# Softmax sums of an attention loop: the reciprocals' way through DRAM, and the place of two reads in the DMA queue

## The chip, the cores and the metric

The kernel runs on one core of one Trainium2 chip. A core has a matrix engine (TensorE, PE in the profile, with its weight loads as PEld), VectorE (DVE), ScalarE (ACT), GpSimd (POOL) and a queue engine, SyncE (SP), which issues nearly all of this kernel's transfers. The metric is the device time in microseconds (us) of one execution. The time before the change is 2631.48 us, the median of three runs (2627.51 to 2632.87).

## The reference

One layer of a diffusion transformer over 1024 latent tokens of width 1024, with 256 context tokens in front: a half-step feed-forward part, then a convolution branch beside an attention branch, merged by gates, then a second feed-forward part and a final norm. All is float32. The change lies in the attention, where 8 query heads in 2 groups read 1280 keys (256 of the context, 1024 latent), each with head width 128:

```
s = einsum('btkgd,blkd->bkgtl', q, k) * HEAD_DIM ** -0.5
p = softmax(s, axis=-1)
o = einsum('bkgtl,blkd->btkgd', p, v)
```

## The kernel before

Products are made from float32 values split into a high and a low part, as high by high, high by low and low by high: three matmuls stand for one product, and each operand costs a cast (ACT or POOL) and a subtraction (DVE or POOL). The kernel runs in stages: first feed-forward part, input projections, heads, attention, the branches' outputs and merge, second feed-forward part. In most stages a planner with a cost model orders the instructions. The attention loop is written out by hand: while `strict` is set, every engine, and SP with its transfers, keeps the order of the program text.

**The loop** has 16 units, one for each head and each half (512) of the queries. A unit has five steps, and step `t` of the loop does four things: scores and exponentials of 128 queries of the current unit (in the unit's first four steps), the turning of two key tiles of 128 of the unit before (`turn`, `placed_parts`), the product with the values for the two tiles turned in the step before (`values`), and some matmuls of the convolution branch's output projection (`fillers`, with their weight and input loads). Other work is put into four places of a step by `later(t, place, ...)`: `first`, `mid`, `after` and `end`, in this order; the fillers run between `after` and `end`. Things put into one place run in the order in which they were put there, unit by unit.

**Turning the probabilities.** The value product needs keys on the partitions. For query tiles 2 and 3 of a unit, and for the context keys, TensorE turns them. For query tiles 0 and 1 the exponentials of the latent keys lie in two tiles `pb` (128 by 1024), and each goes this way (`place`): VectorE turns its 32 by 32 blocks in place; four transfers write it to DRAM as `turned`, in pieces of 64 numbers (256 bytes); one transfer reads it back as `placed`, in pieces of 1024 bytes, with keys on the partitions. Below, the write and the read of a unit's first `pb` are write A and read A, those of the second write B and read B. With `t0` a unit's first step, write A stands at the end of `t0+3` and read A at the first place of `t0+4`; write B stands at the end of `t0+4` and read B at the first place of `t0+5`. `placed` is first used in step `t0+7` (A) and `t0+9` (B).

**The sums.** The exponentials are not divided before the value product. VectorE sums them (`rsum`, 128 partitions by 4 query tiles); `inverse` takes the reciprocals (`rinv`), writes these 512 numbers to DRAM (`rinvd`) and reads them back as one row of 512 on all 128 partitions (`rrow`); `output` multiplies the unit's output, which has queries along the row, by that row on POOL (on VectorE for the last unit). The write of `rinv` stands at the end of `t0+6`, which is step 1 of the next unit, and the row's read at the end of `t0+9`; the product comes in step `t0+12`. In DRAM the row is in the order of the queries, so the write

```
sp.dma_start(out=row.rearrange("(j p) -> p j", p=P), in_=rinv[:])
```

puts down 512 single numbers of 4 bytes.

**SP's queue** takes its transfers in order, and one that waits for its data holds all behind it. A read of something that was written to DRAM waits until the write has landed. Around the change the order for unit `n`, with the fillers' loads (`g`, `raw`, `y`) and stores (`zd`) in between, is: write A(n), read A(n), `rrow`(n-1), write B(n), read B(n), `rinvd`(n), write A(n+1).

Of the kernel before, what the change touches and what calls it, by code (L numbers as in the profile page):

```python
# [18 lines left out]
P = 128  # L19
# [32 lines left out]
def tile_dit_layer(  # L52
# [44 lines left out]
    act, dve, pool, pe, sp = (Engine(e) for e in (nc.scalar, nc.vector, nc.gpsimd, nc.tensor, nc.sync))  # L97
# [11 lines left out]
    def uniq(s):  # L109
        n_tiles[0] += 1  # L110
        return f"{s}_{n_tiles[0]}"
# [4 lines left out]
    def ttile(name, n=512, dt=F32):  # L116
        t = tpool.tile([P, 512], dt, tag="t", name=uniq(name))
        return t[:, :n]

    def small(name, n, dt=F32):  # L120
        return spool.tile([P, n], dt, tag=f"s{n}_{name}", name=uniq(name))
# [64 lines left out]
    def col(name, k=0):  # L186
        o = voff[name] + k
        return cols[:, o : o + 1]
# [856 lines left out]
    def fetch_tokens(ch):  # L1045
        s, o, n = ch
        src = x[0] if s == "l" else ctxt[0]
        toks = []
        for j in range(n // P):
            t = atile("xtok")  # L1050
            load(t[:], src[o + j * P : o + (j + 1) * P, :], True)
            toks.append(t)
        return toks
# [41 lines left out]
    t0 = fetch_tokens(C0)  # L1095
# [47 lines left out]
    for k in range(4):  # L1143
        if k % 2:
            half1.shifted(h0[k][:, 0], k, xh[k])
        else:
            dve.tensor_scalar(
                out=h0[k][:, 0], in0=xh[k], scalar1=gain1["l"][:, k : k + 1], scalar2=modl[:, k : k + 1],
# [131 lines left out]
    for j in range(NH):  # L1280
        half1.side = side(j) if j >= SIDE_FROM else None
        u, c = half1.next_first()
        v, b = half1.second(u)
# [115 lines left out]
    for i in range(KD):  # L1399
# [6 lines left out]
        for ch, bg, gc in mixed():  # L1406
# [4 lines left out]
            for j in (0, 2):  # L1411
# [3 lines left out]
                    out=ya, in0=u[:, a + j - 1 : b + j - 1], scalar=col(f"w{j}", i), in1=ya, op0=ALU.mult, op1=ALU.add  # L1415
# [112 lines left out]
    def q_of(hd, ch):  # L1528
        return q_pairs[hd // 2, ch][:, hd % 2]
# [92 lines left out]
    class Unit:  # L1622
# [84 lines left out]
            matmul(po, vh, pts[:, 1], start=False, stop=(kt == 9))  # L1707

        def inverse(self):
            rinv = small("rinv", 4)  # L1710
            dve.reciprocal(out=rinv[:], in_=self.rsum[:])
            yield
            row = dram.tile([512], F32, name=uniq("rinvd"))
            sp.dma_start(out=row.rearrange("(j p) -> p j", p=P), in_=rinv[:])
            yield
            self.rows = ttile("rrow")
            sp.dma_start(out=self.rows, in_=row.partition_broadcast(P))
            yield

        def output(self, by=None):  # L1720
            of = q_of(self.hd, self.ch)
            v = lambda t, by: t[:, :256].rearrange(by, i=4, q=2)
            act.copy(out=v(of, "p (q i c) -> p q i c"), in_=v(self.po, "p (i q c) -> p q i c"))
            act.copy(out=of[:, 256:], in_=self.po[:, 256:])
            yield
            (by or pool).tensor_mul(out=of, in0=of, in1=self.rows)
            yield

    m_hi, m_lo = {}, {}
# [39 lines left out]
    def later(t, when, f, *args):  # L1769
        todo.setdefault((t, when), []).append((f, args))  # L1770
# [74 lines left out]
    for n, u in enumerate(units):  # L1845
        t0, t1 = n * STEPS_OF_UNIT, (n + 1) * STEPS_OF_UNIT
        if n:
            later(t0 - 2, "mid", u.begin, split_apart)
        for j in range(2):
            place = u.place(j)  # L1850
            later(t0 + 2 + j, "after", run, place, 1)
            later(t0 + 3 + j, "end", run, place, 1)
            later(t0 + 4 + j, "first", run, place, 1)
        inverse, output = u.inverse(), u.output(dve if n == len(units) - 1 else None)
        later(t1 + LAG, "after", run, inverse, 1)
        later(t1 + LAG, "end", run, inverse, 1)
        later(t1 + LAG + 3, "end", run, inverse, 1)
        later(t1 + LAG + 6, "mid", run, output, 1)
        later(t1 + LAG + 6, "end", run, output, 1)
        if n % 2 and n < len(units) - 1:  # L1860
            later(last - 1 + u.hd // 2, "after", split_output, u.hd, C0, True)
            later(last + 1 + u.hd // 2, "after", split_output, u.hd, C1, True)
# [5 lines left out]
    turned = {}  # L1868
# [45 lines left out]
    first = fast.norm0()  # L1914
    fast.gain = norm_gain("gain3", 6, "g3")["l"]
    for ch in (C0, C1):
        o = ch[1]
        for d in range(KD):
# [7 lines left out]
                out=xs(d, ch), in0=ps, scalar=modl[:, 40 + d : 41 + d], in1=xs(d, ch), op0=ALU.mult, op1=ALU.add  # L1926
# [12 lines left out]
        out=gf[:], in0=cols[:, voff["gf"] : voff["gf"] + 8], scalar1=math.sqrt(D), scalar2=None, op0=ALU.mult  # L1939
# [47 lines left out]
    for j in range(NH):  # L1987
# [3 lines left out]
        v, b = fast.second(u)  # L1991
# [81 lines left out]
```

## Time and profile before

| what | value |
|---|---|
| median of three runs | 2631.48 us (2627.51 to 2632.87) |
| the profiled execution, its own time | 2631.88 us |
| its span, first to last instruction | 2630.1 us |
| busy: PE, DVE, ACT, POOL | 2588.5, 2003.6, 1184.4, 605.7 us |
| granted TensorE clock, mean | 0.995 |
| attention: first and last reciprocals of sums | 1457.5 and 1783.8 us of the span |
| DMA: moved, mean rate | 418.27 MB, 159 GB/s |

An instruction's row has its line, engine, operation, the tiles it writes and reads, how many there are, busy time in us, the mean of one in ns, and the engine's idle time just before with what ended it. All of this kernel's instructions go through one helper and so have one line, L90; they are told apart by their tiles. A matmul's end is modelled, so a busy TensorE is not one at its peak. Rows of waits say which engine waited for whom: us in total, how many times, the longest. Rows of a stretch (from:to) have its length, the busy time of PE, PEld, DVE, ACT and POOL with their instructions, the granted clock, the share of time in which the 16 DMA engines were busy, and GB/s. Rows in order of time have start, duration, engine, and in brackets the idle time before and what ended it.

### The profile page before, as it was taken

How to read it: one execution, taken by the hardware profiler on the slowest of the kernel's cores; microseconds unless marked ns; L12 is line 12 of the kernel's file. 1: busy time of each engine (PE TensorE's matmuls, PEld its weight loads, DVE VectorE, ACT ScalarE, POOL GpSimd, SP SyncE). 2: the span in 40 equal slices, each digit the busy share in tenths (PEclk: the TensorE clock that was granted, in tenths of full speed). 3: DMA queues.
4: the chain of work that ended last, by engine and by line, in shares of the span. 5: the costliest groups of instructions: out<-in, count | busy, mean ns of one | idle time of the engine just before them, and what ended most of it. 6: DMA issues, size and time to landing. Idle time of an engine off the chain costs nothing. (4 is left out here: it accounts for less than half of the span.)

```text
span 2630.1 us, 35610 instructions
## 1 busy us (share of the span) xinstructions
PE 2588.5 (98%) x12387; PEld 2152.3 (82%) x12387; DVE 2003.6 (76%) x3381; ACT 1184.4 (45%) x2480; POOL 605.7 (23%) x497
## 2 busy tenths in 40 slices
PE   8999999999999999999999999998999999999998
PEld 5888898888888888888888877876888888888888
DVE  5888876878897879977788776775457786667996
ACT  6533454333554642333345676763237223334553
POOL 0135201221010034333022344432000442321100
PEclk9999999999999999999999999999999999999999
DMA  9666475335973364533523787886425653227831
GB/s 325 205 206 199 141 213 171 121 116 204 309 182 116 129 205 157 175 120 99 198 69 95 136 173 142 153 146 178 156 85 176 193 176 96 89 83 277 199 83 65
DMA packets 470763, 418.27 MB, mean 159 GB/s; under 512 B 100134, under 2 KB 353208, under 8 KB 470584
## 3 DMA queue, kind: packets, MB, share of 16 engines
q1 hardware_dynamic: 462936, 401.33, 51.7%
q0 software_dynamic: 7648, 14.68, 3.3%
q8 instruction: 97, 1.59, 0.3%
q14 instruction: 82, 0.67, 0.1%
HBM read 327.23 MB, written 88.64 MB: 158 GB/s over the span
## 5 line engine op out<-in xcount | busy, mean ns | idle before, releaser
L90 PE MATMUL ps<-r,wl 128*128 128x512 f32 x5196 | 1197.0, 390 | 2.7 <-ACT r L90 1.7
L90 PEld LDWEIGHTS ps<-r,wl 128*128 128x128 f32 x5196 | 972.3, 188 | 205.9 <-ACT r L90 1.9
L90 ACT CAST wl<-sum 128x512 fp32r<-128x512 f32 x218 | 133.9, 621 | 316.6 <-PE ps L90 242.7
L90 ACT CAST wl<-raw 128x512 fp32r<-128x512 f32 x287 | 177.7, 620 | 207.2 <-PE ps L90 157.4
L90 DVE TENSOR_TENSOR wl<-raw,wl 128x512 fp32r<-128x512 f32 x287 | 206.0, 721 | 62.7 <-ACT wl L90 61.2
L90 POOL TENSOR_TENSOR sum<-raw 128x512 f32<-128x512 f32 x55 | 80.9, 1472 | 707.5 <-DVE wl L90 224.3
L90 DVE TENSOR_TENSOR wl<-sum,wl 128x512 fp32r<-128x512 f32 x218 | 193.4, 888 | 42.8 <-ACT wl L90 41.6
L90 DVE TENSOR_REDUCE m<-ps 128x1 f32<-128x512 f32 (+1 forms) x192 | 114.8, 602 | 82.9 <-PE ps L90 65.2
L90 DVE TENSOR_TENSOR u<-u,ps 128x512 f32<-128x512 f32 x186 | 126.7, 681 | 33.8 <-PE ps L90 33.8
L90 DVE SCALAR_TENSOR_TENSOR macc<-rawm,silu_r,macc 128x512 f32<-128x512 f32 x165 | 134.3, 835 | 16.7 <-DMA rawm<-in_w_mod_dram 16.3
L90 ACT CAST rh<-hid 128x512 fp32r<-128x512 f32 x132 | 81.8, 622 | 135.9 <-PE ps L90 110.2
L90 POOL TENSOR_TENSOR pts<-placed,pts 128x256 fp32r<-128x256 f32 x128 | 94.7, 762 | 199.5 <-ACT pts L90 120.5
L90 POOL TENSOR_TENSOR sum<-raw,sum 128x512 f32<-128x512 f32 x55 | 76.6, 1393 | 271.8 <-DVE wl L90 267.3
L90 PE MATMUL ps<-rh,wl 128*128 128x512 f32 x360 | 122.1, 390 | 0.0
L90 PE MATMUL ps<-wh,r 128*128 128x512 f32 x384 | 120.4, 393 | 0.0
L90 ACT CAST wh<-raw 128x512 fp32r<-128x512 f32 (+1 forms) x83 | 66.0, 796 | 111.6 <-PE ps L90 76.8
L90 DVE TENSOR_TENSOR rl<-hid,rh 128x512 fp32r<-128x512 f32 x132 | 90.8, 692 | 26.4 <-ACT rh L90 14.9
L90 PE MATMUL ps<-y,wc 128*128 128x512 f32 x384 | 102.8, 394 | 2.0 <-DVE y L90 1.2
L90 PE MATMUL ps<-rh,wh 128*128 128x512 f32 x300 | 102.3, 389 | 0.0
L90 PE MATMUL ps<-kl,qs 128*128 128x512 f32 x384 | 99.9, 395 | 1.9 <-ACT pb L90 1.8
L90 POOL DMA_DIRECT2D ws<-in_ffn_w_out_dram x30 | 35.5, 1232 | 252.5 <-DMA ws<-in_ffn_w_out_dram 64.2
L90 POOL TENSOR_TENSOR sum<-sum,raw 128x512 f32<-128x512 f32 x55 | 87.0, 1581 | 6.0 <-PE ps L90 4.0
(339 smaller groups left out, 5144.9 us busy)
## 6 DMA issues: line engine op xcount, KB each, us to landing
raw<-in_ffn_w_in_dram SPq DMA_DIRECT2D x131, 512.0 KB
raw<-in_ffn_w_out_dram SPq DMA_DIRECT2D x72, 512.0 KB
rawm<-in_w_mod_dram SPq DMA_DIRECT2D x136, 256.0 KB
raw<-in_w_in_dram SPq DMA_DIRECT2D x64, 512.0 KB
hid<-hd SPq DMA_DIRECT2D x40, 512.0 KB
ucd<-uc SPq DMA_DIRECT2D x33, 512.0 KB
turned<-pb SPq DMA_DIRECT2D x128, 128.0 KB
placed<-turned SPq DMA_DIRECT2D x32, 512.0 KB
```

The lines of the kernel that those rows point to most:

```text
L90: inst = getattr(self.engine, name)(*args, **kw)
```

## The change

Three edits. In `inverse` the four columns of reciprocals are put into columns 0, 32, 64 and 96 of a 128 by 128 tile, which is filled with ones first; VectorE turns its 32 by 32 blocks, after which the numbers lie in partitions 0, 32, 64 and 96, 128 in each; these four rows of 512 bytes are written to DRAM. The row in DRAM is then in the order (i, j, r), where query `j*128 + i*32 + r` is meant, and in `output` the product takes both operands through views that put this right. In the loop, reads A and B move from the first place of their steps to the end of the same steps.

```diff
         def inverse(self):
-            rinv = small("rinv", 4)
-            dve.reciprocal(out=rinv[:], in_=self.rsum[:])
+            turned = ttile("rinv", P)
+            dve.memset(turned, 1.0)
+            dve.reciprocal(out=turned[:, ::32], in_=self.rsum[:])
+            dve.transpose(out=turned, in_=turned)
             yield
             row = dram.tile([512], F32, name=uniq("rinvd"))
-            sp.dma_start(out=row.rearrange("(j p) -> p j", p=P), in_=rinv[:])
+            sp.dma_start(out=row.rearrange("(i f) -> i f", i=4), in_=turned[::32])
             yield
             self.rows = ttile("rrow")
             sp.dma_start(out=self.rows, in_=row.partition_broadcast(P))
...
-            (by or pool).tensor_mul(out=of, in0=of, in1=self.rows)
+            v = lambda t, by: t.rearrange(by, i=4, j=4)
+            of, rows = v(of, "p (j i r) -> p j i r"), v(self.rows, "p (i j r) -> p j i r")
+            (by or pool).tensor_mul(out=of, in0=of, in1=rows)
             yield
...
             place = u.place(j)
             later(t0 + 2 + j, "after", run, place, 1)
             later(t0 + 3 + j, "end", run, place, 1)
-            later(t0 + 4 + j, "first", run, place, 1)
+            later(t0 + 4 + j, "end", run, place, 1)
```

In SP's queue the order becomes: write A(n), the fillers' loads of step `t0+4`, `rrow`(n-1), read A(n), write B(n), the fillers' loads of step `t0+5`, read B(n), `rinvd`(n), write A(n+1).

## The prediction

> **What bounds the kernel now.** The page's head comes first:
>
> ```profile
> span 2630.1 us, 35610 instructions
> PE 2588.5 (98%) x12387; PEld 2152.3 (82%) x12387; DVE 2003.6 (76%) x3381; ACT 1184.4 (45%) x2480; POOL 605.7 (23%) x497
> L90 PE MATMUL ps<-kl,qs 128*128 128x512 f32 x384 | 99.9, 395 | 1.9 <-ACT pb L90 1.8
> ```
>
> TensorE sets the end, so the change is worth what it takes out of TensorE's waits, no more. It touches attention alone, so next I took the busy times of the stretch from the first reciprocals to the last turned keys, then, narrower, the granted clock:
>
> ```profile
> 1457.00:1806.00 349.00, 328.70 (x1647) 267.92 (x1648) 252.62 (x545) 242.12 (x720) 142.48 (x155) 0.98 0.82 147
> ...
> 1584.00:1588.00 4.00, 4.00 (x18) 3.51 (x17) 0.00 (x0) 3.46 (x9) 3.63 (x3) 0.57 0.34 80
> 1747.00:1752.00 5.00, 4.95 (x15) 3.85 (x16) 2.70 (x7) 3.61 (x12) 2.73 (x4) 0.66 0.57 170
> 1788.00:1803.00 15.00, 10.41 (x28) 7.52 (x29) 9.00 (x11) 8.40 (x20) 10.13 (x8) 0.66 0.64 198
> ```
>
> TensorE stands for 349.0 - 328.7 = 20.3 us of this stretch. In three places its clock is lowered as well: 4 x 0.43 + 5 x 0.34 + 15 x 0.34 = 8.5 us of work lost. About 0.6 us of that falls into a wait counted already, so 7.9. Who ended the waits (TensorE's rows, then ScalarE's, then SP's, same stretch):
>
> ```profile
> PE ps L90 <- ACT pts L90: 7.5, 2, 5.0
> PE pt L90 <- DVE pts L90: 6.0, 6, 2.5
> PE ps L90 <- ACT pc L90: 2.9, 3, 1.8
> PE ps L90 <- ACT pb L90: 1.8, 1, 1.8
> PE ps L90 <- DVE y L90: 1.2, 1, 1.2
> PE po L90 <- ACT pts L90: 1.1, 2, 0.7
> ```
>
> ```profile
> ACT pts L90 <- DMA placed<-turned: 37.0, 12, 7.3
> ACT pb L90 <- DMA turned<-pb: 2.7, 1, 2.7
> ```
>
> ```profile
> SPq L90 <- DMA turned<-pb: 145.5, 53, 9.5
> ```
>
> TensorE waits for ScalarE, and ScalarE waits for `placed`, 37.0 us in 12 of 32 reads; while it stands, its exponentials (`pc`, `pb`) stand too. `placed` is late because SP waits 145.5 us for the landing of `turned`. Why that takes so long is seen in SP's order, unit 0 above the dots, units 2 and 3 below:
>
> ```profile
> 1440.01 2.19 SPq L90 DMA_DIRECT2D turned<-pb  x4
> 1444.50 0.39 SPq L90 DMA_DIRECT2D placed<-turned  x1
> ...
> 1501.98 0.38 SPq L90 DMA_DIRECT2D placed<-turned  x1
> 1502.46 0.45 SPq L90 DMA_DIRECT2D rinvd<-rinv  x1
> 1503.96 2.64 SPq L90 DMA_DIRECT2D turned<-pb  x4
> 1515.38 0.38 SPq L90 DMA_DIRECT2D placed<-turned  x1
> 1516.83 0.43 SPq L90 DMA_DIRECT2D rrow<-rinvd  x1
> 1517.36 2.76 SPq L90 DMA_DIRECT2D turned<-pb  x4
> 1523.26 0.38 SPq L90 DMA_DIRECT2D placed<-turned  x1
> ```
>
> Write A of unit 3 ends its issue at 1506.6 and read A starts at 1515.38: 8.8 us to land. Write B, of the same size and shape, takes 1523.26 - 1520.12 = 3.1 us; write A of unit 0, with no write of sums ahead of it, 2.3. What precedes the slow one alone is `rinvd`, 512 pieces of 4 bytes. The DMA's columns say the same:
>
> ```profile
> 1440.00:1445.00 5.00, 4.44 (x21) 3.43 (x20) 3.02 (x6) 3.22 (x9) 2.39 (x1) 1.00 0.62 108
> ...
> 1506.00:1515.00 9.00, 8.55 (x42) 6.43 (x41) 6.74 (x17) 4.74 (x17) 2.19 (x4) 1.00 1.11 46
> 1517.00:1523.00 6.00, 6.00 (x31) 4.86 (x31) 4.47 (x11) 4.98 (x14) 3.13 (x3) 1.00 1.05 324
> ```
>
> After the 4-byte pieces the engines count as fully busy and move 46 GB/s; around write B, as busy, 324. So the small pieces hold up what comes behind them. Two kinds of lateness follow: a read B issued just ahead of `rinvd` is not done for 10.7 us (issued 1501.98, cast at 1512.70), and a read A starts late behind its slow write, then takes 4.1 us (1785.58 to 1789.66, last unit):
>
> ```profile
> 1512.70 0.71 ACT L90 CAST pts<-placed 128x256 fp32r<-128x256 f32 x2 [3.93 <-DMA placed<-turned]
> ...
> 1789.66 0.71 ACT L90 CAST pts<-placed 128x256 fp32r<-128x256 f32 x2 [7.25 <-DMA placed<-turned]
> ...
> 1785.58 0.38 SPq L90 DMA_DIRECT2D placed<-turned  x1
> ```
>
> [...]
>
> **The change part by part.** *The write of four rows.* 16 x 512 = 8192 pieces of 4 bytes become 64 of 512 bytes. No write of this trace has this form; its cost lies between nothing and that of today's write. I take nothing, since four pieces are few beside the 2048 of a write B, which lands in 3.1 us. Write A then lands 2.3 to 3.1 us after its issue instead of 8.8, and read A can start some 6 us earlier; read B is no longer held up. What this releases, term by term:
>
> - TensorE's waits for ScalarE, 7.5 + 1.1 + 2.9 + 1.8 = 13.3 us: all taken. Bounds: half of it, if reads stay at the edge, to all.
> - Of the 6.0 us for VectorE's `pts`, the wait of 2.5 us: VectorE's row shows that it had stood 7.82 us for ScalarE's casts of `oh`, which stood behind `placed` in ScalarE's order. The other five are VectorE's own queue. Bounds 0 to 6.0.
>
> ```profile
> 1792.42 5.27 DVE L90 TENSOR_TENSOR ol<-q,oh 128x512 fp32r<-128x512 f32 x3 [7.82 <-ACT oh L90]
> ```
>
> - The clock, 7.9 us: each of the three places follows such a wait. [...]
> - What waits don't show. A matmul's row is 395 ns, but 384 of them add only 99.9 us of busy time, 260 ns each: in a gap the modelled end covers some 0.13 us. For the 9 waits above, 1.2 us; bounds 0 to 2.
>
> [...]
>
> Sum of gains: 13.3 + 2.5 + 7.9 + 1.2 = 24.9 us.
>
> *The work added on VectorE and POOL.* The rows nearest to it:
>
> ```profile
> L90 DVE RECIPROCAL rinv<-rsum x16: 167/168/171, 1457.5 to 1783.8; 128x4 f32<-128x4 f32 x16
> L90 DVE STREAM_TRANSPOSE pb<-pb 128x1024 f32<-128x1024 f32 x32 | 39.5, 1235 | 0.0
> L90 POOL TENSOR_TENSOR q<-q,rrow x15: 1282/1297/1734, 1481.3 to 1794.3; 128x512 f32<-128x512 f32 x15
> L90 POOL TENSOR_TENSOR hsw<-xb,rope x48: 456/790/1716, 1291.6 to 1423.1; 128x256 f32<-128x256 f32 x32, 128x128 f32<-128x128 f32 x16
> ```
>
> The reciprocal stays, 0.17 us. The turn of 128 columns costs between 1235/8 = 154 ns and that plus the 168 of a small operation; I take 0.2. The fill, not in the trace on this engine at this size, is put at 0.05 to 0.3 by the same rows; I take 0.15. That is 0.35 us for a unit, 5.6 in all, on an engine busy for 252.62 of 349 us:
>
> ```profile
> DVE m L90 <- PE ps L90: 58.7, 93, 4.3
> 1544.50:1566.25 21.75, 20.55 (x108) 16.89 (x107) 19.34 (x39) 16.86 (x50) 10.00 (x10) 1.00 0.81 144
> ```
>
> VectorE's next maxima of scores (`m`) queue behind it, and these have 58.7 us of waiting for TensorE to spare. Where VectorE is dense (19.34 of 21.75 us here; two or three of 16 units) it shows: 3 x 0.35, about 1.0 us; bounds 0 to 5.6. POOL's product runs over 32-number pieces; the rotary product, whose view is also of 32s, takes 790 ns for mostly half the size, so at most 1.6 against 1.3, and POOL is busy for 142 of 349 us: nothing.
>
> *The reads at the end of a step.* Read A now stands behind `rrow` and the fillers' loads, 0.4 to 0.5 us of issue each and at most two or three of them, and these go out while SP would have waited for write A. So up to about 1 us later in the order, against 6 gained. A step is (1783.8 - 1457.5)/15/5 = 4.35 us; from the end of `t0+4` to the use in `t0+7` there are two steps, 8.7, for the 4.1 of a read; for read B three. Behind read A wait write B and all later transfers, which are earlier for the same reason. A gain by itself: none; loss: none while write A is quick, 4 us if it isn't (last rival).
>
> Net 24.9 - 1.0 = 23.9 us. The profiled execution took 2631.88 us (1.8 around its span), so 2631.88 - 23.9 = **2608 us**; it lies 0.4 above the runs' median, which changes nothing.
>
> **The rivals.** *VectorE takes over:* the waits go, but the dense units and the last two hit its queue, with the 6.0 us of `pts` waits kept and the added 5.6 exposed. 13.3 + 6.0 (part of the clock) - 5.6 = 14: 2618. For it: 19.34 of 21.75 us in a unit. Against: the 58.7 us.
>
> *More than the sum:* all 20.3 us of waits, the clock and the hidden ends go, 20.3 + 7.9 + 2 = 30: 2602, less if the order behind the loop, which the planner makes anew, happens to be better. Against: `y` (1.2) and VectorE's own queue are not touched.
>
> *No change:* the lateness of `placed` moves elsewhere, or the four rows, each from a single partition, land as slowly as the single numbers did: the change doesn't do what it says. Then row and reads are late as now, 2631. For it: no row shows such a write. Against: 46 GB/s goes with 4-byte pieces alone.
>
> *Slower:* write A is slow by itself, above all from its 256-byte pieces with reads around it, and the reads now stand 1 us further back. It decides from where write A still needs over 8 us to land: read A is at its deadline there in the 12 units where ScalarE waits now. 12 x 1 us on ScalarE, of which TensorE feels 13.3/37 = a third, 4 us, and the 5.6 of VectorE: 2641. For it: 53 waits for `turned`, not 16, so writes B have some too. Against: unit 0 and the 324 GB/s.
>
> **How the numbers follow.** Forecast 0.62 (its own range 2601 to 2614); VectorE takes over 0.16; more than the sum 0.08; no change 0.06; slower 0.08. 0.2%, 5.3 us, is about what a measurement of this kernel tells from no change. The first three are faster, 0.86; no change 0.06; slower 0.08. The range reaches from the case of more than the sum, with 3 us for the planner (2602 - 3 = 2599), to the case of VectorE with the 13.3 halved, its lower bound (2618 + 7 = 2625).
>
> **What would show it.** Right: SP's waits for `turned` fall from 145.5 us to under 90; write A lands within 3 to 4 us; ScalarE's waits for `placed` fall from 37 us to under 5; no stretch with the DMA busy at 46 GB/s; the clock at 1.00 throughout attention; TensorE's idle time there falls from 20 to 4 to 6 us. Wrong: `pts` waits on VectorE above 6 us (it took over); read A still 8 us or more behind write A (slow by itself); a VectorE that waits for a buffer at the fill; a later stage that changed by over 3 us, which would be the planner's doing.

## The result, and the profile after

The changed kernel takes 2608.38 us, the median of four runs (2606.43 to 2609.92), against 2632.18 us before in the same set: a ratio of 0.9908, 95% interval 0.9888 to 0.9929. That is 23.8 us less; 23.9 were forecast, 2608 us as the time.

The head of the page after:

```profile
span 2608.2 us, 35685 instructions
PE 2579.6 (99%) x12387; PEld 2150.7 (82%) x12387; DVE 2011.1 (77%) x3413; ACT 1182.6 (45%) x2480; POOL 602.1 (23%) x497
```

Its busy time by stretches, first for attention from the first reciprocals to the last turned keys (here 325 us long), then for the last 15 us of that; the columns are those of the prediction's rows:

```profile
1460.00:1785.00 325.00, 318.36 (x1648) 264.61 (x1647) 260.02 (x577) 241.26 (x719) 142.89 (x155) 0.99 0.64 165
1770.00:1785.00 15.00, 11.59 (x48) 9.06 (x49) 11.54 (x19) 9.23 (x22) 10.38 (x9) 0.89 0.62 200
```

TensorE's waits in attention, by what ended them (sum in us, how many, the longest):

```profile
PE pt L90 <- DVE pts L90: 6.1, 5, 2.1
PE ps L90 <- DVE y L90: 1.2, 1, 1.2
PE pt L90 <- DVE rinv L90: 0.2, 1, 0.2
```

The stretch was 349 us and TensorE stood for 20.3 of it; now it stands for 325.0 - 318.4 = 6.6. All its waits for ScalarE are gone, and ScalarE has no wait for `placed` left. What stays is VectorE's. The clock is lowered in one place, 15 x 0.11 = 1.7 us of work instead of 8.5.

SP's order for unit 3 is to be held beside the rows of the same unit before:

```profile
1502.23 0.50 SPq L90 DMA_DIRECT2D rinvd<-rinv  x1
1506.58 2.84 SPq L90 DMA_DIRECT2D turned<-pb  x4
1509.46 0.54 SPq L90 DMA_DIRECT2D g<-gcd  x1
1510.05 0.74 SPq L90 DMA_DIRECT2D y<-yd  x1
1510.88 0.38 SPq L90 DMA_DIRECT2D rrow<-rinvd  x1
1511.80 0.37 SPq L90 DMA_DIRECT2D placed<-turned  x1
1512.27 4.18 SPq L90 DMA_DIRECT2D turned<-pb  x4
```

Write A ends its issue at 1509.4 and read A starts at 1511.8, 2.4 us later instead of 8.8, though three loads went out in between. SP's waits in the changed kernel (sum in us, how many, the longest):

```profile
SPq L90 <- DVE rsum L90: 106.3, 29, 6.9
SPq L90 <- DMA turned<-pb: 51.1, 48, 2.7
```

Its busy time by stretches, here for the time behind the write of the sums, with the share and rate of the DMA engines as the last two columns:

```profile
1506.50:1512.00 5.50, 5.50 (x29) 4.55 (x28) 5.09 (x13) 4.85 (x17) 1.67 (x3) 1.00 0.74 141
```

Where the engines counted as fully busy at 46 GB/s, they now move 141 GB/s at a share of 0.74. SP's wait for `turned` fell from 145.5 to 51.1 us. It now waits for VectorE (106.3 us, put down to `rsum`, the last thing VectorE does in such a step): it is ahead of the engines, where it was behind them.

Where the 21.9 us between the two spans (2630.1 and 2608.2) are: from the first to the last reciprocals 326.3 us became 310.0 (1460.4 to 1770.4), 16.3 less; from there to the end 846.3 became 837.8, 8.5 less. Nearly all of this lies in attention: up to its last turned keys (1806.0 and 1784.8) it takes 24.1 us less, what follows 0.7. The first reciprocals came 2.9 us later. This last belongs to the profiled execution and not to the change: the clock was lowered longer at the start, as the same stretch before and after shows:

```profile
20.00:80.00 60.00, 55.06 (x260) 40.67 (x259) 43.98 (x85) 40.36 (x71) 0.00 (x0) 0.94 0.89 281
```

```profile
20.00:80.00 60.00, 54.72 (x251) 40.90 (x250) 41.96 (x81) 39.99 (x71) 0.00 (x0) 0.89 0.87 272
```

60 x 0.05 = 3 us.

### The profile page after: what moved, and what is told of

Read it like the earlier page. It is cut to its first block, busy times and chain, and to the rows that moved or that the text cites. A ratio compares the mean times of both kernels' runs of the same rounds, so it can differ in the third digit from the quotient of the medians.

```text
span 2608.2 us, 35685 instructions
## 1 busy us (share of the span) xinstructions
PE 2579.6 (99%) x12387; PEld 2150.7 (82%) x12387; DVE 2011.1 (77%) x3413; ACT 1182.6 (45%) x2480; POOL 602.1 (23%) x497
```

## The experiments

Below, the hold is the delay that the write of single numbers brings to what stands behind it. Three sets were run on three chips, each beside the kernel before on the same chip. The first set has the two edits together and apart and the later split in the tail, the second the first three of the small writes and VectorE's added work, the third the rest. The kernel before takes 2644.31, 2640.38 and 2651.66 us there. The changed kernel itself ran on the first of these chips alone (2609.40 us); on the other two, kernels with a harmless spare write stand for it (2608.15, and 2607.70 and 2609.43 us). So kernels are compared within a set, by their ratio to the kernel before or with such a kernel on the same chip.

### The two edits together and apart

The changed kernel again:

> The changed kernel itself, beside the one before and the parts of it on the same chip. Both theories: 0.991 of the kernel before, some 24 us less, as measured first.

2609.40 us (2608.97 to 2610.80), ratio 0.9870 (0.9857 to 0.9883). On this chip the gain is 35 us, more than expected, because the kernel before is slower here.

The four-row write alone:

```diff
-            later(t0 + 4 + j, "end", run, place, 1)
+            later(t0 + 4 + j, "first", run, place, 1)
```

> The four-row write alone; reads A and B stay at the first place of their steps. Theory (the 4-byte pieces are the cause): all but 1 us of the gain, 23 to 25 us less than before, SP's waits for turned some 20 us above those of the changed kernel (it now stands where it could have issued loads), no effect on TensorE. Rival (the place of the reads matters, since a waiting read holds the loads behind it): at least a third of the gain lost, 16 us less than before or fewer.

2608.84 us, ratio 0.9869 (0.9856 to 0.9882): the whole gain. SP waits 74.5 us for `turned`, 23 more than in the changed kernel, and the time does not show it. Once the write is mended, the reads' place is worth nothing that can be measured.

The reads' place alone, with the sums as single numbers:

```diff
-            later(t0 + 4 + j, "first", run, place, 1)
+            later(t0 + 4 + j, "end", run, place, 1)
```

> The reads' new place alone; the sums are still written as 512 single numbers. Theory: write A still needs 8 to 9 us to land, read A stands up to 1 us further back, so 0 to 6 us slower than before. Rival (the place of the reads matters): at least a third of the gain, 8 us faster or more.

2636.62 us (2629.77 to 2640.77), ratio 0.9968 (0.9955 to 0.9980): some 8 us faster than before (7.7 by the medians), at the rival's bound in microseconds, though under a third of this chip's 35, and outside the theory's range. SP's order at unit 3 in this kernel:

```profile
1502.20 0.45 SPq L90 DMA_DIRECT2D rinvd<-rinv  x1
1504.80 2.19 SPq L90 DMA_DIRECT2D turned<-pb  x4
1507.03 0.63 SPq L90 DMA_DIRECT2D g<-gcd  x1
1507.70 0.72 SPq L90 DMA_DIRECT2D y<-yd  x1
1514.81 0.32 SPq L90 DMA_DIRECT2D rrow<-rinvd  x1
1516.46 0.37 SPq L90 DMA_DIRECT2D placed<-turned  x1
```

And SP's waits in it:

```profile
SPq L90 <- DMA turned<-pb: 63.1, 54, 3.2
SPq L90 <- DMA rinvd<-rinv: 50.9, 7, 8.4
```

Write A is as slow as ever: 1516.46 - 1506.99 = 9.5 us. The wait now falls partly on `rrow`, which waits for the landing of the single numbers themselves, and the loads `g` and `y` go out before it instead of behind it. Together SP waits 114 us on these two instead of 146. So a place behind the loads does help while the write is slow; the gains of the two edits don't add up (35 and 8 us each by itself, 35 together).

### The small pieces put back

The changed kernel keeps its four rows; a spare write of 512 single numbers, which nobody reads, goes out behind them.

```diff
             sp.dma_start(out=row.rearrange("(i f) -> i f", i=4), in_=turned[::32])
+            spare = dram.tile([512], F32, name=uniq("spare"))
+            sp.dma_start(out=spare.rearrange("(j p) -> p j", p=P), in_=self.rsum[:])
```

> The changed kernel with one more write for each unit, just behind that of the four rows: the 128 by 4 sums as 512 single numbers of 4 bytes to 2 KB of DRAM that nothing reads. Nothing waits for it; it only stands in the DMA engines ahead of write A. Theory: write A again needs 8 us or more, ScalarE waits for placed again, 15 to 25 us slower than the changed kernel. Rival (in the kernel before it was the wait for the row's landing or VectorE's order that cost, not the pieces): within 3 us of the changed kernel.

2629.23 us, 21 above the kernel with the numbers apart (next) on the same chip; ratio to before 0.9960 (0.9945 to 0.9975). Write A takes 8.4 us to land, as in the kernel before (the median over units 1 to 15, here and below), and ScalarE waits for `placed` again:

```profile
ACT pts L90 <- DMA placed<-turned: 25.8, 11, 9.2
```

So the pieces themselves hold up what stands behind them, with no wait on their landing and no order of VectorE's in it. The ratio is also that of the reads' new place alone (0.9968), as it should be if the single numbers are all that the four rows take away.

A landing counted from the end of the issue doesn't show the hold in every unit. In units 1, 5, 9, 13 and 15 of the kernel before it is only 2.6 to 4.4 us, but there the issue of write A's four parts takes 7.5 to 10.3 us. Counted from the end of the small write to read A, every unit of the kernel before needs 12 to 15 us, and every unit of the kernel with the numbers apart 7 to 9.

The same 512 numbers, each 512 bytes from the next:

```diff
+            spare = dram.tile([512, 128], F32, name=uniq("spare"))
+            sp.dma_start(
+                out=spare.rearrange("(j p) c -> p j c", p=P)[:, :, 0:1],
+                in_=self.rsum[:].rearrange("p (j o) -> p j o", o=1),
+            )
```

> As the kernel with the spare write of single numbers, but the 512 numbers go 512 bytes apart, so that no two lie in one block of 512 bytes. Theory in its plain form (the size of a piece costs): as slow as with the numbers packed, 15 to 25 us above the changed kernel. Rival (what costs is that neighbours lie in one block of memory): under 5 us above the changed kernel.

2608.15 us (2606.82 to 2610.81): nothing lost, and write A lands in 2.4 us, the median over the units, against 8.4 packed. Neither the size of these pieces nor the number of them costs by itself; the plain form of the theory falls. What holds here is that single numbers lie packed.

Unit 1 shows that not only writes are held. In both kernels a load of weights (`raw`, 512 KB) is issued right behind the spare write, and write A 3.3 us after it. The stretch of 10 us that begins 2 us after the spare write's issue, first with the numbers packed, then apart:

```profile
1464.60:1474.60 10.00, 10.00 (x55) 8.42 (x54) 8.34 (x18) 8.62 (x26) 5.78 (x6) 1.00 0.20 32
```

```profile
1464.40:1474.40 10.00, 10.00 (x54) 8.45 (x54) 8.35 (x18) 8.60 (x26) 5.82 (x6) 1.00 0.79 177
```

With the numbers packed next to nothing passes, the load included, although the engines count as busy for a fifth of the time only. The trace's records of single pieces name the wrong ones too: the 4-byte pieces take 8 to 10 ns each in attention, packed or apart, while of the 256-byte pieces behind them about a thousand take over 300 ns (up to 4.6 us) with the numbers packed, and none with them apart.

Fewer and larger pieces, packed, without VectorE's turn:

```diff
-            turned = ttile("rinv", P)
-            dve.memset(turned, 1.0)
-            dve.reciprocal(out=turned[:, ::32], in_=self.rsum[:])
-            dve.transpose(out=turned, in_=turned)
+            rinv = small("rinv", 4)
+            dve.reciprocal(out=rinv[:], in_=self.rsum[:])
...
-            sp.dma_start(out=row.rearrange("(i f) -> i f", i=4), in_=turned[::32])
+            sp.dma_start(out=row.rearrange("(p j) -> p j", p=P), in_=rinv[:])
...
-            v = lambda t, by: t.rearrange(by, i=4, j=4)
-            of, rows = v(of, "p (j i r) -> p j i r"), v(self.rows, "p (i j r) -> p j i r")
+            of, rows = of.rearrange("p (j q) -> p j q", j=4), self.rows.rearrange("p (q j) -> p j q", j=4)
```

> No turn on VectorE: the reciprocals go to DRAM as 128 pieces of 16 bytes, partition by partition, and the product reads the row with a step of 4 numbers. Theory in its plain form (number of small pieces): a quarter of the pieces, a quarter of the hold, write A lands in 4 to 5 us, still before read A's deadline: within 3 us of the changed kernel, less 0 to 1 for VectorE. Rival (any piece far below 256 bytes holds, by its size and by sharing a block): write A 7 us or more, 10 to 20 us slower than the changed kernel.

2610.94 us (2610.33 to 2612.56), 2.8 above the kernel with the numbers apart, on the same chip, with ranges that just overlap. The pieces of 16 bytes hold nothing, although they lie packed: write A lands in 2.4 us, the median over the units, not in 4 to 5. What this version may lose is in the product, which steps through the row:

```profile
L90 POOL TENSOR_TENSOR q<-q,rrow x15: 1547/1558/1992, 1483.7 to 1773.0; 128x512 f32<-128x512 f32 x15
L90 DVE TENSOR_TENSOR q<-q,rrow x1: 1058/1058/1058, 1791.9 to 1791.9; 128x512 f32<-128x512 f32 x1
```

1558 ns against 1294 on POOL and 1058 against 682 on VectorE in the changed kernel. That this makes the 2.8 us was not tried by itself.

Three more spare writes ask what packed means. First, packed, but partition by partition:

```diff
+            spare = dram.tile([512], F32, name=uniq("spare"))
+            sp.dma_start(out=spare.rearrange("(p j) -> p j", p=P), in_=turned[:, ::32])
```

> [...] If neighbours in one small block hold each other up whoever writes them: slow as the packed spare write before, some 2629 us, write A 8 us or more. [...]

2643.34 us (2634.18 to 2650.05), ratio 0.9963 (0.9944 to 0.9982): slow, so the order of the numbers doesn't matter, and neighbours from one partition hold as neighbours from different ones do. Whether one engine wrote them stays open, for no row tells which engine serves which partition. In time this is 14 us above the 2629 expected, but that figure is from another chip; the ratio is the same. Then with gaps, `dram.tile([512, 2])` and `dram.tile([512, 16])` in place of the `[512, 128]` above:

> The spare write with 8 bytes from one number to the next, in the order of the write in the kernel before: 8 numbers lie in 64 bytes, all from neighbouring partitions. If blocks of 64 bytes or less and several engines are the cause, quick (write A 2.4 us, within 3 us of the changed kernel); if neighbours in a block cost whoever writes them, or the block is larger than 64 bytes, slow (write A over 4 us).

2609.43 us (two runs): quick. Write A took 2.7 us, the median over the units, but up to 4.9 in single ones; a little of the hold is left.

> The spare write with 64 bytes from one number to the next: 8 numbers lie in 512 bytes. If the block is of 512 bytes: slow, write A over 4 us. If it is of 64 bytes or less: quick, write A 2.4 us, within 3 us of the changed kernel.

2607.70 us (two runs): quick, write A 2.4 us.

SP's rows of unit 3 in the kernel with the numbers packed partition by partition, and in the one with 8 bytes from number to number:

```profile
1504.83 0.54 SPq L90 DMA_DIRECT2D spare<-rinv  x1
1505.80 2.69 SPq L90 DMA_DIRECT2D turned<-pb  x4
...
1517.44 0.37 SPq L90 DMA_DIRECT2D placed<-turned  x1
```

```profile
1504.57 0.44 SPq L90 DMA_DIRECT2D spare<-rsum  x1
1508.37 2.19 SPq L90 DMA_DIRECT2D turned<-pb  x4
...
1512.92 0.37 SPq L90 DMA_DIRECT2D placed<-turned  x1
```

8.9 us to land against 2.4. The two differ in the order of the numbers as well as in the gap of 4 bytes; packed in the second one's order (the first spare write above, on another chip), unit 3's write A took 9.5 us. And the DMA in the stretch behind the spare write, in the same two kernels:

```profile
1508.00:1517.00 9.00, 9.00 (x49) 7.54 (x48) 6.52 (x16) 5.73 (x19) 3.09 (x5) 1.00 1.25 93
```

```profile
1508.00:1517.00 9.00, 9.00 (x48) 7.59 (x47) 6.96 (x17) 6.41 (x21) 3.53 (x5) 1.00 0.79 180
```

Busy in full at 93 GB/s, against four fifths busy at 180. Whether packed 4-byte writes hold because the numbers touch or because the region is small these runs don't tell: 8 bytes apart no two numbers touch, but they also cover 4 KB instead of 2.

### The kernel before, where it is slower

> The kernel before once more, for its profile on a chip where it takes longer (2640 us and more in two sets of runs here, against 2631 in the first). Theory: what differs is the time that write A takes to land, above 8.4 us in the middle, and not the stages outside attention.

2654.91 us here (2648.28 to 2658.70). Attention in this kernel on this chip, from the first reciprocals to the last turned keys:

```profile
1461.00:1830.00 369.00, 334.67 (x1649) 273.25 (x1650) 252.47 (x546) 242.92 (x721) 141.61 (x155) 0.95 0.83 139
```

TensorE stands for 34.3 us of it instead of 20.3, and the clock is 0.95 instead of 0.98; write A needs 9.2 us to land, the median over the units, instead of 8.4, and up to 11.6. Of the 24.9 us between the spans of the two profiled executions, 19.4 are attention's; 4.2 lie ahead of it and 1.3 behind. So the theory holds in the main. The hold is somewhat longer here and far more of it reaches TensorE; why, and what the 4.2 us ahead are, isn't shown.

### VectorE

The fill done twice and the turn three times, which gives the same numbers:

```diff
-            dve.memset(turned, 1.0)
+            dve.memset(turned, 1.0)
+            dve.memset(turned, 1.0)
...
-            dve.transpose(out=turned, in_=turned)
+            dve.transpose(out=turned, in_=turned)
+            dve.transpose(out=turned, in_=turned)
+            dve.transpose(out=turned, in_=turned)
```

> The changed kernel with the fill done twice and the turn three times, which gives the same numbers: about 0.8 us more on VectorE for each unit, 12.6 us in all. Forecast's theory (hidden but for the dense units and the tail, 1.0 of 5.6 us): 2 to 4 us slower than the changed kernel. Rival (VectorE takes over): 8 to 13 us slower.

2613.08 us (2611.61 to 2613.91), 3.7 above the changed kernel on the first set's chip and 4.9 above the kernel with the numbers apart on the same chip. One more fill and two more turns are 16 x (0.165 + 2 x 0.311) = 12.6 us; by the medians about a third shows. Not all of it need be VectorE's. Between the profiled executions of the two edits and of this kernel, attention became only 0.9 us longer (324.3 and 325.2), or 2.6 without the 1.7 us that the clock, lowered here nowhere in attention, gives back; the rest lies ahead of attention. So a fifth to a third shows. VectorE doesn't take over, but hides less than was thought.

What is left in the tail, the end of the attention loop, where VectorE splits the outputs of seven heads:

```diff
-            later(last + 1 + u.hd // 2, "after", split_output, u.hd, C1, True)
+            later(last + 3 + u.hd // 2, "after", split_output, u.hd, C1, True)
```

> The changed kernel, with the splits of the outputs' second halves (C1) put two steps later at the end of the loop, so that VectorE has at most three of them in a step instead of four. In the changed kernel TensorE waits 6.1 us for VectorE's pts in the tail. Theory (VectorE's own queue is what is left there): two of these waits shrink, 1 to 3 us less than the changed kernel, its clock dip in the tail gone or not. Rival (POOL's work beside it holds VectorE): no change within 1 us.

2606.67 us (2605.04 to 2607.76), ratio 0.9858 (0.9846 to 0.9871), 2.7 us under the changed kernel on the same chip, and the ranges of the runs don't touch. TensorE's waits for `pts` fall from 6.1 to 2.9 us, and the clock is not lowered in attention any more. Attention in this kernel, to the last turned keys:

```profile
1460.00:1782.00 322.00, 317.69 (x1648) 263.47 (x1648) 258.94 (x576) 240.13 (x718) 142.37 (x155) 1.00 0.66 167
```

And its row of TensorE's waits for `pts`:

```profile
PE pt L90 <- DVE pts L90: 2.9, 5, 1.0
```

This version is faster than both kernels.

## Why the prediction was right, point by point

**The slow write.** Right. Write A lands in 2.4 us (2.3 to 3.1 forecast), SP's waits for `turned` are 51.1 us (under 90), those of ScalarE for `placed` are gone (under 5). "The small pieces hold up what comes behind them" was argued from one order of events; the spare write that is put back shows it. But the reason that the prediction had in mind, many small pieces, is not the whole: 512 pieces of 4 bytes with gaps cost nothing. Three of the prediction's own signs were missed by little: the clock is not at 1.00 throughout attention (0.89 in its last 15 us), TensorE's idle time is 6.6 us and not 4 to 6, and the `pts` waits are 6.1 us, where more than 6 was to mean that VectorE took over.

**The four rows cost nothing.** Right, as far as the waits show: SP has no wait for the row's landing in the changed kernel.

**13.3 us of waits for ScalarE.** Right; none of the four rows is left.

**2.5 us of `pts`.** Wrong. The term said that the wait of 2.5 us, which came after VectorE had stood for ScalarE, would go. The sum of these waits is 6.1 us, where it was 6.0. VectorE's rows in the tail of the changed kernel:

```profile
1767.22 3.02 DVE L90 TENSOR_TENSOR ol<-q,oh 128x512 fp32r<-128x512 f32 x4
1770.21 0.17 DVE L90 MEMSET rinv<- 128x128 f32 x1
1770.41 0.18 DVE L90 RECIPROCAL rinv<-rsum 128x4 f32<-128x4 f32 x1
1770.63 0.31 DVE L90 STREAM_TRANSPOSE rinv<-rinv 128x128 f32<-128x128 f32 x1
1770.87 0.72 DVE L90 TENSOR_TENSOR pts<-pt,pts 128x256 fp32r<-128x256 f32 x2
1771.51 5.05 DVE L90 TENSOR_TENSOR ol<-q,oh 128x512 fp32r<-128x512 f32 x3
```

TensorE's rows there, with two of the waits:

```profile
1771.31 0.77 PE L90 MATMUL pt<-ident,pl 128*128 128x128 f32 x4 [2.12 <-DVE pts L90]
1776.94 0.77 PE L90 MATMUL pt<-ident,pl 128*128 128x128 f32 x4 [2.10 <-DVE pts L90]
```

In the kernel before, the wait ahead of the first of these was shorter, and so were the four splits that VectorE did before it:

```profile
1784.32 0.77 PE L90 MATMUL pt<-ident,pl 128*128 128x128 f32 x4 [0.97 <-DVE pts L90]
1781.38 2.48 DVE L90 TENSOR_TENSOR ol<-q,oh 128x512 fp32r<-128x512 f32 x4
```

The three splits take 5.05 us without any wait for ScalarE ahead of them (5.27 before, behind the 7.82), so the 2.10 behind them was VectorE's own all along. And the wait that was 0.97 is 2.12, 1.15 more: the new fill and turn, 0.5 us together, stand in front of `pts` just there, and the four splits took 3.02 us instead of 2.48; why they did isn't known. The splits put later took 3.2 us off these waits, which shows whose they are.

**The clock, 7.9 us.** Nearly: 8.5 us of lowered clock became 1.7, so 6.8 went; the place that stays (0.89 over the last 15 us) is behind the two waits above, of 2.12 and 2.10 us.

**What waits don't show, 1.2 us.** Too small. The waits' rows and the clock give (20.3 - 6.6) + (8.5 - 1.7) = 20.5 us, and attention gave 24.1. Taken from the matmuls' starts (time to the next start, less the median one for that shape, gaps in the records included), TensorE's loss over attention fell from 37.6 to 13.8 us, 23.8 less. So 3 to 4 us lay under the modelled ends. This and the missing 2.5 offset each other; that the time came out within a microsecond is partly luck. So is the chip: on the one of the first set the same change gave 35 us, because the kernel before is slower there.

**VectorE's work, 0.35 us a unit.** It is 0.165 for the fill and 0.311 for the turn, 7.6 us in all instead of 5.6, and by the experiment a fifth to a third of such work shows, some 1.5 to 2.5 us instead of 1.0. The turn's price was taken near the lower bound; the upper one, 0.32, was right. POOL's product takes 1294 ns, as before (1297), so nothing there, as forecast.

**The reads' place: no gain, and 4 us lost if write A stays slow.** The first half was right (2608.84 us without it, 2609.40 with it). The second was wrong in sign: with the slow write it gains some 8 us. The step that failed counted only read A's own delay, up to 1 us; it had said itself that the loads ahead of it would go out while SP waits, and priced that at nothing, which is the part that is left to explain a gain. By which of the loads TensorE gains the 8 us is not settled: there is no profile of the kernel before from that chip.

**The rivals.** VectorE takes over: no, though its queue is what remains. No change, because four rows from single partitions land slowly: no. More than the sum: no; `y`'s 1.2 us and VectorE's queue stayed, as was said against it. Slower, with 256-byte pieces slow by themselves: no; with the four rows, writes of 256-byte pieces land in 2.4 us (A) and about 3.1 (B).

## What to carry to other kernels

Look at what stands ahead of a slow transfer in the DMA engines, and not only at the transfer: here a write of 2 KB made the next 512 KB six to seven microseconds late (8.4 to 9.5 us to land instead of 2.4), and both the rows of waits and the records of single pieces named only the innocent one. The two cures for one wait did not add here (35 and 8 us each by itself, 35 together): the one at its root made the other worth nothing, and the next bound (VectorE's queue in the tail, 2.7 us) was then worth a look of its own. A wait put down to an engine that had just stood for another can still be that engine's own, as the 2.10 us in the tail were.

## What the runs showed of the hardware that was not expected

Packed writes of single 4-byte numbers to DRAM hold up what stands behind them, a load too, for some 6 to 7 us (write A takes 8.4 to 9.5 us to land, medians over the units of five profiles, instead of 2.4), in either order of the numbers. With 8, 64 or 512 bytes from number to number, or as packed pieces of 16 bytes, they don't (2.7, 2.4, 2.4 and 2.4 us). The kernel before took 2631 to 2655 us by the chip; the changed kernel and those with a harmless spare write took 2608 to 2609 us on all four, though no single one of them ran on all. That a longer hold makes this difference was seen in one pair of profiles (8.4 and 9.2 us) and not tried by itself.
